# Rebuilding the last mixer tile and the router of a mixture-of-experts block, with unread matmuls between the router's steps

## The chip, the cores and the metric

The kernel runs on one core of a Trainium2 chip. The metric is the device time of one execution in microseconds, lower being better. Engines are named as in the profile: PE (TensorE matmuls), PEld (its weight loads), DVE (VectorE), ACT (ScalarE), POOL (GpSimd), SP (SyncE, which here only issues transfers).

## The reference, cut to what matters

One layer of an encoder, on x of 1024 tokens by 1024 channels, all in fp32. The part around the change:

```python
mix_out = jnp.einsum('bsd,de->bse', z, w_o[l])
x = x + gate_m[:, None, :] * mix_out
h2 = modulate(rms_norm(x, g_norm_moe[l]), shift_f, scale_f)      # h * (1 + scale) + shift
moe_out = expert_choice_moe(h2, w_router[l], ...)
x = x + gate_f[:, None, :] * moe_out
return rms_norm(x, g_final)

def expert_choice_moe(h, w_router, b_router, w_gate_e, w_up_e, w_down_e):
    probs = jax.nn.softmax(h @ w_router + b_router, axis=-1)     # 16 experts
    vals, idx = lax.top_k(jnp.swapaxes(probs, 1, 2), cap)        # each expert picks its 128 best tokens
    xe = h[idx]
    y = (jax.nn.silu(xe @ w_gate_e) * (xe @ w_up_e)) @ w_down_e  # 1024 -> 2048 -> 1024
    return scatter_add(y * vals)
```

No expert can start before every token's probability is known, since each picks its tokens from all 1024.

## The kernel before, in words

Every large product is done in three matmuls of fp32r operands: each operand is split into a rounded part (`hi`, a copy on ACT) and the rest (`lo`, a subtraction on DVE), and hi x hi, hi x lo, lo x hi are summed in PSUM (`split`, L92 and L93; `mm3`, `mm3x`).

The work around the change comes in this order.

**The mixer's last product** (`mix_out`): eight tiles of 128 tokens. A tile takes eight k steps of six matmuls of 512 columns (L105, L108, L111), both column halves in each step. Behind it the tile's x is added (L814), squared (L819), and stored; `rstd` goes over DVE and POOL (L656, L658); the row is scaled and modulated on DVE (L828, L830) and stored in `h2_d` by a POOL-issued transfer (L831). The router's work of a tile runs inside the next one, ahead of its k step 6: `turn` transposes x (L739) and splits it, `logits` multiplies with the router weights (L747, L749) and takes the softmax (L752 to L760), and `compare` ranks the tokens of experts 0 and 1 against all earlier ones (L859 to L878): comparisons on DVE, counted by small matmuls on PE (L862). For the last tile, 7, transposes and logits come after its own products.

**The router's end** (`run`): `compare` of tile 7 for expert 0, then `pick`: a one-hot table on DVE (L968), eight small matmuls (L975), the index (L981), and the gather of 128 rows of `h2_d` (L985) by an indirect POOL transfer. `turn` (the method) transposes the gathered rows (L1002) and splits them into `xh` and `xl`. The ranking of expert 1 and the search for the other 14 run as side work during expert 0.

**Sixteen experts** (`expert`): the weights come as units of 1 MB into a ring of raw buffers (`fetch`, L1018; 7 + 5 + 3 = 15 of them), and `unit` splits each in two halves of 1024 columns into `whi` and `wlo`, of which the pool `mwsp` has NWS = 3 each. The first three `wlo` are queued on DVE behind the index (L1037); all others go through `split`. An expert takes four column blocks: `up` twice (L1155 to L1157, gate and up), `put` (transposes of the product, L1077), `down` (L105 to L111). The next expert's gather is issued in the second block, its rows are turned between the two halves of the last `down`, and after that `ys` is scaled (L1126) and added into `x2_d` by an indirect transfer (L1127). After the last expert the rows are normalised (`final`).

The order on each engine isn't written out: the framework orders instructions by a simulated schedule with the traced order as priority, each engine then runs its queue in that order, and `issue_after(i)` queues what a block traces behind instruction i on i's engine. On the chip a waiting instruction holds up all behind it on its engine.

## Time and profile before

| | |
|---|---|
| median of 3 runs | 1964.37 us (1959.64 to 1964.53) |
| profiled execution | 1961.4 us, span 1959.6 us |
| PE busy | 1881.2 us (96%) |
| DVE busy | 1608.2 us (82%) |
| ACT busy | 1169.2 us (60%) |
| POOL busy | 141.7 us (7%) |
| mean granted clock of TensorE | 0.984 of full speed |
| HBM traffic | 549.03 MB, mean 280 GB/s |

Busy shares are of the span. The page's second part cuts the span into 40 slices of 49 us; PE shows 9 tenths in all but the first, the slice around 760 us, and the last. The mixer's product ends shortly before 754 us, the experts' products run from 783 to 1950 us. A busy PE isn't one at its peak, as matmuls are pipelined: distances from start to start tell more than durations.

### The profile page before, as it was taken

The numbers are of one execution on the slowest core, as the hardware profiler recorded it, in microseconds if no ns is written. First come the engines' busy times: TensorE is split into PE (matmuls) and PEld (weight loads), VectorE is DVE, ScalarE is ACT, GpSimd is POOL, SyncE is SP. The second block draws the span as 40 slices with busy tenths as digits, with TensorE's granted clock in tenths as the row PEclk, the third lists the DMA queues.
The fourth block names the chain that finished last, engine by engine and source line by source line (L and its number), as shares of the span: only waits on it lengthen the run. The fifth ranks groups of instructions, "written<-read, shape, count | busy, mean of one in ns | idle before, by whom it ended". The sixth has DMA issues, their size and how long they took to land.

```text
span 1959.6 us, 24141 instructions
## 1 busy us (share of the span) xinstructions
PE 1881.2 (96%) x8677; PEld 1505.6 (77%) x8677; DVE 1608.2 (82%) x2083; ACT 1169.2 (60%) x1402; POOL 141.7 (7%) x127
## 2 busy tenths in 40 slices
PE   6999999999999996999999999999999999999985
PEld 5788888777788874777888888777777877777764
DVE  5976669676753777999999999899999899998985
ACT  5533233433411422777777777777777777777784
POOL 1000000000131111000000000000000000000011
PEclk9999999999999997999999999999999999999997
DMA  8322224464764945999999999999999999999981
GB/s 296 128 65 65 86 86 151 160 223 171 258 240 121 328 148 208 361 327 375 373 369 384 376 370 356 384 363 356 387 359 360 381 365 361 381 369 350 378 309 79
DMA packets 245261, 549.03 MB, mean 280 GB/s; under 512 B 12644, under 2 KB 51652, under 8 KB 245140
## 3 DMA queue, kind: packets, MB, share of 16 engines
q1 hardware_dynamic: 230160, 496.07, 70.0%
q0 software_dynamic: 14128, 51.18, 8.2%
q8 instruction: 68, 1.11, 0.2%
q14 instruction: 53, 0.43, 0.1%
q10 hardware_dynamic: 852, 0.24, 0.1%
HBM read 507.61 MB, written 39.86 MB: 279 GB/s over the span
## 4 chain that ended last, share of the span: by engine, by line
PE 79%; DVE 10%; issue 6%; ACT 2%; DMA 1%; POOL 1%; POOLq 0%; SPq 0%; ACTq 0%; DVEq 0%
PE pb L314 9%; PE u L1157 6%; PE pa L314 6%; DVE wlo L93 6%; PE pc L314 6%; PE u L1155 6%; PE u L1156 6%; PE a L1157 5%; PE a L1156 4%; PE a L1155 4%; PE y L105 4%; PE y L108 4%; PE y L111 4%; PE mm L111 3%; PE mm L105 3%
## 5 line engine op out<-in xcount | busy, mean ns | idle before, releaser
L93 DVE TENSOR_TENSOR wlo<-raw,whi 128x1024 fp32r<-128x1024 f32 x765 | 912.1, 1225 | 64.9 <-ACT whi L92 52.4
L92 ACT ACTIVATE whi<-raw 128x1024 fp32r<-128x1024 f32 x765 | 803.1, 1060 | 216.0 <-PE y L111 78.1
L1157 PE MATMUL a<-wlo,xh 128*128 128x512 f32 x512 | 208.5, 407 | 10.3 <-DVE wlo L93 9.5
L1155 PE MATMUL a<-whi,xh 128*128 128x512 f32 x512 | 204.4, 399 | 6.8 <-ACT whi L92 6.8
L1157 PE MATMUL u<-wlo,xh 128*128 128x512 f32 x512 | 204.7, 400 | 2.4 <-DVE wlo L93 1.8
L1155 PE MATMUL u<-whi,xh 128*128 128x512 f32 x512 | 204.3, 399 | 0.2 <-ACT whi L92 0.2
L1156 PE MATMUL a<-whi,xl 128*128 128x512 f32 x512 | 203.4, 397 | 0.2 <-DVE xl L93 0.2
L1156 PE MATMUL u<-whi,xl 128*128 128x512 f32 x512 | 202.7, 396 | 0.0
L108 PE MATMUL y<-wlo,hth 128*128 128x512 f32 x508 | 162.6, 401 | 2.6 <-DVE wlo L93 2.6
L105 PE MATMUL y<-whi,hth 128*128 128x512 f32 x508 | 160.8, 397 | 2.4 <-ACT whi L92 2.4
L111 PE MATMUL y<-whi,htl 128*128 128x512 f32 x508 | 158.6, 393 | 0.0
L1157 PEld LDWEIGHTS a<-wlo,xh 128*128 128x128 f32 x512 | 97.0, 190 | 44.5 <-DVE wlo L93 23.3
L92 ACT ACTIVATE wh<-s 128x512 fp32r<-128x512 f32 x80 | 50.3, 631 | 134.9 <-PE pc L314 73.4
L1157 PEld LDWEIGHTS u<-wlo,xh 128*128 128x128 f32 x512 | 96.7, 189 | 28.9 <-DVE wlo L93 6.1
L1155 PEld LDWEIGHTS a<-whi,xh 128*128 128x128 f32 x512 | 97.5, 190 | 27.1 <-ACT whi L92 7.2
L1156 PEld LDWEIGHTS a<-whi,xl 128*128 128x128 f32 x512 | 97.4, 190 | 23.4 <-DVE xl L93 0.7
L1156 PEld LDWEIGHTS u<-whi,xl 128*128 128x128 f32 x512 | 96.7, 189 | 21.9
L1155 PEld LDWEIGHTS u<-whi,xh 128*128 128x128 f32 x512 | 96.8, 189 | 21.0 <-ACT whi L92 0.6
L111 PEld LDWEIGHTS y<-whi,htl 128*128 128x128 f32 x508 | 95.8, 189 | 21.0
L105 PEld LDWEIGHTS y<-whi,hth 128*128 128x128 f32 x508 | 93.8, 189 | 22.0 <-ACT whi L92 2.9
L108 PEld LDWEIGHTS y<-wlo,hth 128*128 128x128 f32 x508 | 92.0, 189 | 22.0 <-DVE wlo L93 4.5
L92 ACT ACTIVATE wh<-ld 128x512 fp32r<-128x512 f32 x68 | 42.4, 629 | 88.1 <-issue 36.1
(523 smaller groups left out, 3157.2 us busy)
## 6 DMA issues: line engine op xcount, KB each, us to landing
raw<-in_w_gate_e_dram SPq DMA_DIRECT2D x128, 1024.0 KB, 8.4
raw<-in_w_up_e_dram SPq DMA_DIRECT2D x126, 1024.0 KB, 7.6
raw<-in_w_down_e_dram SPq DMA_DIRECT2D x126, 1024.0 KB, 8.2
ld<-in_w_ada_dram SPq DMA_DIRECT2D x48, 512.0 KB, 5.0
ld<-in_w_in_dram SPq DMA_DIRECT2D x44, 512.0 KB, 4.6
sg_d<-q POOLq DMA_DIRECT2D x8, 1024.0 KB, 5.0
ld<-sg_d SPq DMA_DIRECT2D x16, 512.0 KB, 4.3
x<-in_x_dram SPq DMA_DIRECT2D x8, 512.0 KB, 5.1
```

Of the source, the lines that this page charges most:

```text
L92: self.nc.scalar.activation(hi, src, AF.Copy)
L93: self.nc.vector.tensor_tensor(lo, src, hi, op=OP.subtract)
L105: nc.tensor.matmul(o, lhsT=lh, rhs=rh, start=first, stop=False)
L108: nc.tensor.matmul(o, lhsT=lh, rhs=rl, start=False, stop=False)
L111: nc.tensor.matmul(o, lhsT=ll, rhs=rh, start=False, stop=last)
L314: nc.tensor.matmul(o, lhsT=x[:, k, :], rhs=y[:, k, :], start=first and k == 0 and i == 0, stop=last and k == 3 and i == 2, skip_group_chec ...
L1155: nc.tensor.matmul(o, lhsT=lhs[0], rhs=rhs[0], start=first, stop=False)
L1156: nc.tensor.matmul(o, lhsT=lhs[1], rhs=rhs[0], start=False, stop=False)
L1157: nc.tensor.matmul(o, lhsT=lhs[0], rhs=rhs[1], start=False, stop=last)
```

## The change

- **The last mixer tile** goes by column halves: 24 matmuls for columns 0 to 511, then 24 for the others. Its first half of x is added, squared, transposed and multiplied with the router weights inside the second half.
- **Router work spread**: in the other tiles the work for the tile before stands at three places, `side(0)` (compare of the tile before that), `side(2)` (turn), `side(4)` (logits and softmax), instead of all ahead of step 6. The router weights are negated, so that softmax needs no subtraction ahead of Exp. `compare` takes both experts at once, copies its row on ACT, and stops at a `yield` between the comparisons and the counts.
- **Rows unmodulated**: `h2_d` gets x times rstd, one ACT instruction (`norm`); for tile 7 SP issues both stores, the rows first. Scale and shift are applied after the gather, in the method `turn`, where they are one value per partition: for the first expert on ACT and DVE side by side straight from PSUM, for the others by four ACT instructions a half into `xf`, a copy to `xh` and a subtraction to `xl`.
- **Buffers**: `mwsp` has NWB = 6 of `whi` and `wlo` each; the raw ring is 7 + 4 + 1 = 12. NWS stays 3 where it says which `wlo` are queued behind the index.
- **Later**: `ys` and its scatter are traced after the first unit pair of the next expert (`left`); the load of `g_final` after the last expert's first `up`.
- **Unread matmuls**: `warm` issues n matmuls of the identity with itself, fp32, 128 columns, whose result nobody reads, queued behind a named PE instruction: 2, 5 and 10 at the end of `mix_out`, 4 and 7 around the counts of tile 7, 18 after the index's matmuls.

```diff
-NRA, NRB, NRC, NWO = 7, 5, 3, 6
-NWS = 3
+NRA, NRB, NRC, NWO = 7, 4, 1, 6
+NWS, NWB = 3, 6
...
+    def warm(self, psum, n):
+
+        t = psum()
+        with self.tc.issue_after(self.pe):
+            for _ in range(n):
+                self.nc.tensor.matmul(t[:, 0:P], lhsT=self.ident, rhs=self.ident, start=True, stop=True)
...
+        def norm(x2, h2, ss, ts, eng):
+            nc.vector.tensor_tensor(ss[:, 0:1], ss[:, 0:1], ss[:, 1:2], op=OP.add)
+            rs = self.rstd(pool, ss[:, 0:1], "y")
+            nc.scalar.activation(h2, x2, AF.Copy, scale=rs)
+            eng.dma_start(out=self.h2_d[ts, :], in_=h2)
+            self.afterld = eng.dma_start(out=self.x2_d[ts, :], in_=x2).ins
+            return rs
...
+            for n in range(2):
+                cs = slice(512 * n, 512 * n + 512)
+                for k in range(KD):
+                    if n == 0 and k % 2 == 0:
+                        side(k // 2)
+                    if n == 1 and k == 0:
+                        side(4)
+                    if n == 1 and k == 3:
+                        xt = turned()
+                        turn(x2, xt, 0)
+                    if n == 1 and k == 5:
+                        cmp = self.compare(t - 1, range(NCMP), psum)
+                        next(cmp)
+                    if n == 1 and k == 7:
+                        pl = psum()
+                        logits(pl, xt, 0)
+                    self.mm3([ps[:, cs]], (zh[:, k, :], zl[:, k, :]), [(self.wo[0][:, k, cs], self.wo[1][:, k, cs])],
+                             first=(k == 0), last=(k == KD - 1))
+                add_x(x2, ps, n)
+                if n == 0:
+                    sumsq(x2, h2, ss, n)
...
+            next(cmp, None)
+            self.warm(spare, 2)
+            turn(x2, xt, 1)
+            self.warm(spare, 5)
+            sumsq(x2, h2, ss, 1)
+            rs = norm(x2, h2, ss, ts, nc.sync)
+            logits(pl, xt, 1)
+            self.warm(spare, 10)
+            softmax(t, rs, pl)
...
-            self.split(xh[:, 4 * hf:4 * hf + 4, :], xl[:, 4 * hf:4 * hf + 4, :], pt)
+            hs = slice(4 * hf, 4 * hf + 4)
+            f = pool.tile([P, 4, P], F32, name="xf")
+            for k in range(4):
+                a, b = (self.vc[:, j + 4 * hf + k:j + 4 * hf + k + 1] for j in (16, 0))
+                if first:
+                    nc.scalar.activation(xh[:, 4 * hf + k, :], pt[:, k, :], AF.Identity, scale=a, bias=b)
+                    nc.vector.tensor_scalar(f[:, k, :], pt[:, k, :], a, b, op0=OP.mult, op1=OP.add)
+                else:
+                    nc.scalar.activation(f[:, k, :], pt[:, k, :], AF.Identity, scale=a, bias=b)
+            if not first:
+                nc.scalar.activation(xh[:, hs, :], f, AF.Copy)
+            nc.vector.tensor_tensor(xl[:, hs, :], f, xh[:, hs, :], op=OP.subtract)
...
+                if self.left:
+                    self.left.pop()()
...
-        gwsp, self.wsp = pool("mwsp", "right", bufs=NWS)
+        gwsp, self.wsp = pool("mwsp", "right", bufs=NWB)
...
-        self.compare(p, psum, ST - 1, 0)
+        cmp = self.compare(ST - 1, (0,), psum)
+        next(cmp)
+        self.warm(lambda: self.pau.tile([P, 512], F32, name="a"), 4)
+        for _ in cmp:
+            pass
+        self.warm(lambda: self.pau.tile([P, 512], F32, name="a"), 7)
```

## Rows read from the trace of the kernel before

**Rows 1.** Windows, one late expert: us, engines' busy (instructions), PEclk, DMA share, GB/s.

```profile
1283.50:1354.80 71.30, 70.47 (x322) 56.24 (x321) 64.65 (x64) 55.08 (x59) 3.30 (x2) 1.00 1.03 374
```

**Rows 2.** Page, part 5: line, engine, shapes, count | busy us, mean ns | idle.

```profile
L93 DVE TENSOR_TENSOR wlo<-raw,whi 128x1024 fp32r<-128x1024 f32 x765 | 912.1, 1225 | 64.9 <-ACT whi L92 52.4
L92 ACT ACTIVATE whi<-raw 128x1024 fp32r<-128x1024 f32 x765 | 803.1, 1060 | 216.0 <-PE y L111 78.1
```

**Rows 3.** Timeline, PE: start, us, engine, line, operation [idle before <-releaser].

```profile
753.12 0.63 PE L111 MATMUL mm<-woh,zl 128*128 128x512 f32 x2
...
783.70 0.80 PE L1156 MATMUL a<-whi,xl 128*128 128x512 f32 x1 [0.17 <-DVE xl L93]
...
786.69 0.39 PE L1157 MATMUL a<-wlo,xh 128*128 128x512 f32 x1
```

**Rows 4.** Two-microsecond windows in the router, columns as in rows 1.

```profile
758.00:760.00 2.00, 0.00 (x0) 0.00 (x0) 2.00 (x4) 0.90 (x1) 0.00 (x0) 0.79 1.03 346
...
774.00:776.00 2.00, 0.00 (x0) 0.00 (x0) 2.00 (x3) 0.00 (x0) 0.41 (x1) 0.50 0.04 17
```

**Rows 5.** Timeline, tile 7's rstd and second half, POOL, ScalarE and VectorE.

```profile
757.16 0.55 POOL L658 TENSOR_TENSOR yrs<-yms,neghalf 128x1 f32<-128x1 f32 x1 [7.78 <-DVE yms L656]
757.36 0.60 ACT L92 ACTIVATE hth<-mm 128x512 fp32r<-128x512 f32 x1 [0.26 <-PE mm L739]
...
758.55 0.68 DVE L93 TENSOR_TENSOR htl<-mm,hth 128x512 fp32r<-128x512 f32 x1
```

**Rows 6.** Timeline, counts of tile 6 and probabilities of tile 7.

```profile
760.22 0.32 PE L862 MATMUL sm<-onesb,cmp 128*128 128x1 bf16 x6 [2.90 <-DVE cmp L859]
...
768.32 0.23 DVE L760 TENSOR_SCALAR prob<-lg,se 128x16 f32<-128x16 f32 x1
```

**Rows 7.** Timeline, index and gather of expert 0.

```profile
773.72 0.16 DVE L981 SCALAR_TENSOR_TENSOR idx<-r 128x1 int32<-128x1 f32 x1
...
775.59 1.60 POOL L985 DMA_INDIRECT xg<-h_d,idx  x1 [7.12 <-DVE res L892]
```

**Rows 8.** Chain that ended last, from 740 to 810: start, us, what.

```profile
767.90 6.65 DMA h_d<-h
...
775.59 4.95 DMA xg<-h_d,idx
```

**Rows 9.** Timeline, fp32 matmuls of 128 columns among others at full clock.

```profile
40.95 3.08 PE L142 MATMUL sm<-diag,x 128*128 128x128 f32 x24
```

**Rows 10.** Line 985, the gathers of all experts.

```profile
DMA to landing us min/median/max: 4.9/7.9/9.0
```

**Rows 11.** ScalarE by groups (columns as rows 2), 641 to 654.

```profile
L92 ACT ACTIVATE zh<-ya 128x128 fp32r<-128x128 f32 x2 | 0.5, 302 | 5.0 <-DVE ya L610 5.0
```

**Rows 12.** PE's waits, 600 to 760: us in total, times, longest.

```profile
PE mm L105 <- ACT zh L92: 1.1, 1, 1.1
```

**Rows 13.** Timeline, first unit of two experts, late and early pattern.

```profile
1356.84 0.39 PE L1155 MATMUL a<-whi,xh 128*128 128x512 f32 x1
1357.08 0.40 PE L1156 MATMUL a<-whi,xl 128*128 128x512 f32 x1
1358.13 0.50 PE L1157 MATMUL a<-wlo,xh 128*128 128x512 f32 x1 [0.66 <-DVE wlo L93]
...
1075.24 0.39 PE L1156 MATMUL a<-whi,xl 128*128 128x512 f32 x1
1075.81 0.50 PE L1157 MATMUL a<-wlo,xh 128*128 128x512 f32 x1 [0.18 <-DVE wlo L93]
```

**Rows 14.** Timeline, turn for the next expert, early (with its first matmul), late.

```profile
1068.58 1.04 PE L1002 MATMUL tp<-ident,xg 128*128 128x128 f32 x8
...
1072.22 0.40 PE L1155 MATMUL a<-whi,xh 128*128 128x512 f32 x1
...
1349.44 0.60 PE L1002 MATMUL tp<-ident,xg 128*128 128x128 f32 x4
```

**Rows 15.** Timeline, last expert.

```profile
1910.56 0.79 PE L1155 MATMUL a<-whi,xh 128*128 128x512 f32 x1 [6.76 <-ACT whi L92]
```

More of the change, by code (lines that the diff above doesn't have):

```diff
@@ new lines, in side @@
+        def side(n):
+            if prev is None:
+                return
+            t, x2, rs = prev
+            if n == 0 and t:
+                for _ in self.compare(t - 1, range(NCMP), psum):
+                    pass
+            if n == 2:
+                hold["xt"] = turned()
+                for hf in range(2):
+                    turn(x2, hold["xt"], hf)
+            if n == 4:
+                pl = psum()
+                for hf in range(2):
+                    logits(pl, hold["xt"], hf)
+                softmax(t, rs, pl)
@@ L801, in mix_out @@
             ps = self.psm.tile([P, D], F32, name="mm")
-            for k in range(KD):
-                if k == 6 and prev is not None:
-                    logits(t - 1, prev[1], *turn(prev[0]))
-                    for e in range(NCMP):
-                        self.compare(self.cmpp, lambda: self.pss.tile([P, 512], F32, name="sm"), t - 1, e)
-                self.mm3([ps[:, 0:512], ps[:, 512:1024]], (zh[:, k, :], zl[:, k, :]),
-                         [(self.wo[0][:, k, n:n + 512], self.wo[1][:, k, n:n + 512]) for n in (0, 512)],
-                         first=(k == 0), last=(k == KD - 1))
@@ L856, in compare @@
         pc = psum()
-        if t:
-            m = pool.tile([P, (ST - 1) * P], BF16, name="cmp", bufs=2)
-            nc.vector.tensor_scalar(m[:, 0:n], self.prow[:, e, 0:n], p, 0.0, op0=OP.is_ge, op1=OP.add,
-                                    accum_out=cnt[:, 0:1])
-            for i in range(t):
-                nc.tensor.matmul(pc[:, P + i:P + i + 1], lhsT=m[:, i * P:(i + 1) * P], rhs=self.onesb[:, 0:1],
-                                 start=True, stop=True)
-        nc.tensor.transpose(pc[:, 0:P], p.to_broadcast([P, P]), self.ident)
@@ L877, in compare @@
-        nc.vector.tensor_tensor(place[:, t:t + 1], place[:, t:t + 1], cnt[:, 1:2], op=OP.add)
-        last = nc.vector.tensor_tensor(place[:, t:t + 1], place[:, t:t + 1], cnt[:, 2:3], op=OP.add)
-        if t == ST - 1:
-            self.after = last.ins
-            nc.vector.tensor_copy(self.pos[:, :, e], place)
+        row = pc[:, 0:ne * P].rearrange("p (e s) -> p e s", e=ne)
+        num = pc[:, 256:256 + 8 * ne].rearrange("p (e t) -> p e t", e=ne)
+        p = [self.prob[:, t, e:e + 1] for e in es]
@@ new lines, in compare @@
+        for i in range(ne):
+            self.pe = nc.tensor.transpose(row[:, i, :], p[i].to_broadcast([P, P]), self.ident).ins
+        if not last:
+            nc.scalar.activation(self.prow[:, e0:e0 + ne, n:n + P], row, AF.Copy)
+        ms = []
+        for i, e in enumerate(es):
+            w = n if last else n + P
+            m = pool.tile([P, (ST - 1) * P], BF16, name="cmp", bufs=2)
+            nc.vector.tensor_scalar(m[:, 0:w], self.prow[:, e, 0:w], p[i], 0.0, op0=OP.is_ge, op1=OP.add,
+                                    accum_out=cnt[:, 0, i:i + 1])
+            ms.append(m)
@@ new lines, in compare @@
+        for i, e in enumerate(es):
+            own = pool.tile([P, P], BF16, name="own", bufs=2)
+            r = row[:, i, :] if last else self.prow[:, e, n:n + P]
+            nc.vector.scalar_tensor_tensor(own, in0=r, scalar=p[i], in1=self.upper, op0=OP.is_equal, op1=OP.mult,
+                                           accum_out=cnt[:, 1, i:i + 1])
+            if last:
+                own = pool.tile([P, P], BF16, name="own", bufs=2)
+                nc.vector.tensor_scalar(own, r, p[i], 0.0, op0=OP.is_ge, op1=OP.add, accum_out=cnt[:, 2, i:i + 1])
@@ new lines, in compare @@
+        yield
+        for i in range(ne):
+            for j in range(t):
+                self.pe = nc.tensor.matmul(num[:, i, j:j + 1], lhsT=ms[i][:, j * P:(j + 1) * P],
+                                           rhs=self.onesb[:, 0:1], start=True, stop=True).ins
+        if t:
+            nc.vector.tensor_tensor(place[:, :, 0:t], place[:, :, 0:t], num[:, :, 0:t], op=OP.subtract)
+        own = place[:, :, t]
+        if last:
+            nc.vector.tensor_tensor(cnt[:, 0, :], cnt[:, 0, :], cnt[:, 2, :], op=OP.add)
@@ L883, in weights3 @@
+        nc.vector.tensor_tensor(cnt[:, 0, :], cnt[:, 0, :], cnt[:, 1, :], op=OP.subtract)
+        self.after = nc.vector.tensor_tensor(own, own, cnt[:, 0, :], op=OP.add).ins
     def weights3(self, pool, e0, e1):
@@ L1326, in run @@
                 next(side)
-        picked = self.turn(mp, *picked)
+        picked = self.turn(mp, *picked, first=True)
+        self.left = []
         for e in range(NE):
```

204 lines of the change are left out of this document (100 added, 104 removed).

## The prediction

> **What bounds the kernel now.** I read the page's first two parts, then two-microsecond windows around their dip, then the timeline and the chain of waits there, last the expert stage by windows and timeline. TensorE is the bound nearly everywhere: its tenths stand at nine but for the dip around 760 and the last slices. In the expert stage (783 to 1950) a late expert takes 71.3 us, of which PE is busy 70.47 and VectorE 64.65 [rows 1]; nearly all of VectorE's and ScalarE's time goes to splitting weights, 1.225 and 1.060 us for each half unit [rows 2]. So PE sets the pace, with a few small stalls. The dip is the router: the last mixer matmuls start at 753.12 and end at 753.75 (call it T0); the first expert's second matmul, the first that needs `xl`, starts at 783.70, T0 + 29.95 [rows 3]. Between them runs one serial chain, with PE mostly waiting; the granted clock is 0.79 in 758 to 760 and 0.50 in 774 to 776 [rows 4]: TensorE sits at 1.2 instead of 2.4 GHz when the experts begin. From 783.70 to 786.69 [rows 3] it starts 7 matmuls, where 0.23 us apart (the distance at full clock in rows 13) would take 1.6: 1.4 us lost to the clock.
>
> **The chain before.** The last copy and subtraction of tile 7's transposed half end at 759.23, POOL's power for rstd beside them [rows 5]. Then PE waits 2.90 us for the comparisons of tile 6, whose counts stand ahead of tile 7's logits, and the probabilities end at 768.55, T0 + 14.8 [rows 6]. Ranking and picking end with the index at 773.88, T0 + 20.1; the gather starts only at 775.59 [rows 7], because the store of the modulated rows was issued at 767.90 and took 6.65 us; the gather itself took 4.95 [rows 8], with the DMA engines all but idle at its start (share 0.04) [rows 4].
>
> **The change, router part.** Times from T0', the new end of the last mixer matmul.
> T0' moves later: 4 transposes, 2 of compare, 8 logits matmuls of tile 7 and some 5 of tile 6 that trailed T0 now come before it: 19 instructions at no more than 0.128 us (an fp32 matmul instruction of 128 columns at full clock, 3.08 / 24 [rows 9]) are 2.4; most have fewer columns, so I take 2.1.
> Step 1: compare of tile 6 now stands in front of the add, and VectorE works in order. Its two long and two short comparisons end between 0.15 (the latency of the add's own matmul) and 0.85 after T0'; I take 0.85, as they are traced first. Add 0.68, as long as the subtraction of the same width [rows 5]: 1.55. Four transposes and their latency 0.6, copy 0.60, subtraction 0.68 [rows 5]: 3.5. Eight logits matmuls at most 1.0: 4.6.
> Step 2, beside it: Square and its sum 0.8 after the copy, two tiny steps, POOL 0.55 [rows 5]: rstd at 4.65. Softmax: three short VectorE steps of 0.23 at most [rows 6], then Exp behind the new scaling of the row (1024 columns, 1.06 [rows 2], traced ahead of it), two short steps: probabilities at 6.6, 8.2 earlier than before.
> Step 3: ranking and picking take 5.33 before (768.55 to 773.88) [rows 6, 7]; the small copy of places goes, unread matmuls add 0.3 (below), the order of the few adds changes: 5.0 to 5.3, index at 11.6 to 11.9.
> Step 4: six buffer pairs for split weights instead of three. Only the first three weight subtractions are held behind the index; the next three, 1.225 each [rows 2], may fall into gaps of this chain. Bounds 0 and 3.7; I take 1.3, since the gaps they fill are partly idle: 13.1.
> Step 5: the row store goes out at about 5.8, first on SP's queue, so the 1.7 us before the gather vanish. But x2's store, four weight units and gf follow on that queue: some 5.2 MB, 15 us at the 346 GB/s of such a prefetch [rows 4], still moving at 13. The gather took 4.95 alone; over all 16 it has 4.9/7.9/9.0 (min, median, max) [rows 10], the others beside weight traffic. I take 7.9: 21.0.
> The Trainium skill (DMA: Bandwidth & Descriptors, Queues, rings and completion order) says that each DMA engine goes round the queues that hold work, so POOL's queue gives the gather no priority; 7.9 against 4.95 agrees.
> Step 6: turn of the first expert: transposes 0.6, four 128-column activations of 0.302 [rows 11] with VectorE's twins beside them, subtraction 0.69: 2.6, so the second matmul is at T0' + 23.6.
> Unread matmuls: 46 calls of two instructions, as fp32 matmuls are here, 0.26 us a call [rows 9]: the batches of 2, 5, 10, 4, 7, 18 take 0.5, 1.3, 2.6, 1.0, 1.8, 4.6. Their covers are the waits above (about 1, 1.4, 2.0, 1.2, 1.8, 8): at full clock they cost 0.3. They keep PE busy to about T0' + 17; then 4 us stay empty, so I count the clock as half saved: 0.7 of 1.4.
> Sum: 29.95 - 23.6 - 2.1 + 0.7 = 5 us gained. Bounds: 10.5 (add at once, no fillers, gather 4.95, full clock) and about 0 (all fillers, gather 9.0, clock lost).
>
> **Mixer tiles 0 to 6.** Four VectorE instructions a tile and three broadcast loads go, one ScalarE scaling comes. PE is the bound there and waits for ScalarE 1.1 us once, for a split behind a load [rows 12]: between 0 and 1.1, I take 0.5 gained. The stores of x2 and rows now both wait for rstd in POOL's queue: nobody reads them before the gather.
>
> **Experts.** At a boundary PE waits for `wlo`: 1357.08 to 1358.13 is 1.05 where 0.23 is usual, so 0.82; in the early pattern 1075.24 to 1075.81, 0.34 [rows 13]. Read alike over the stage: five times 0.34, ten times about 0.8, twice 0.25 more in seven experts, 1.6 in expert 1: 14 us or somewhat more. The cause: three buffers, about 4 us of PE work, against xl, ys and h together on VectorE. Six double the lead, and ys moves behind the next expert's first unit; VectorE has the slack to build the lead (64.65 of 71.3 [rows 1]). So up to 14 gained.
> Against it: the turn. Before, two copies of 0.6 on ScalarE. Now per half four activations of 0.302 [rows 11], a copy of 0.6, and a single buffer `xf`, which the second half may write only after VectorE's subtraction of the first; behind that wait, on in-order ScalarE, stand weight splits, and behind them PE. In all 0.4 + 1.2 + 0.6 + (0 to 1.2 until VectorE is free) + 0.7 + 1.2 + 0.6 + 0.7 = 5.4 to 6.6 to the last `xl`. In the early pattern the transposes start at 1068.58 and the next expert at 1072.22 [rows 14]: the first half is needed after 3.9 (takes 2.9 to 4.1), the second after 6.7. With a split of 1.06 in between, a stall of 0 to 1.5. In the late pattern the first half's transposes start at 1349.44 [rows 14], 7.4 us before the seventh matmul of the next expert at 1356.84 [rows 13], so some 6 before its first: nearly nothing. I take 0.45 x 15 = 7 lost. Net 7 gained; bounds 14 gained and 8 lost.
> The Trainium skill (VectorE: DVE Perf Modes, section on the TRN2 errata) wants tiles of 512 elements or more, as each ScalarE or VectorE instruction pays a fixed cost; by its table four 128-column activations from PSUM would take 1.0 us (an estimate), 1.2 by the row. It speaks against this turn.
>
> **Tail.** PE stands 6.76 us for `whi` at 1910.56 [rows 15], ScalarE being busy with final norms. Three more half units ahead are worth up to 4.2 us of PE, but the ring shrinks from 15 to 12, so the x2 rows load later and the norms start later. Between 5 gained and 3 lost; 1.5 gained.
>
> **Sum.** 5 + 0.5 + 7 + 1.5 = 14 off the profiled execution's 1961.4: 1947.4. The median of the runs is 3.0 above that execution: 1950.
>
> **The rivals.**
> Everything fits (20%): the lead removes all stalls, the turn is hidden, gather and clock go well: 9 + 1 + 13 + 4 = 27: 1937. For it: VectorE's slack and the late pattern; against it: the prefetch beside the gather.
> The turn eats the lead (16%): the experts gain nothing, the rest 7: 1957, and 1961 if the router gives little. For it: 5.4 to 6.6 us of turn with 3.6 before the next expert.
> The unread matmuls become the chain (10%): if the clock falls all the same, a call takes twice 0.26, the batches of 5, 10, 4, 7 overrun their covers by about 1, 3, 1, 2 us, and the router gains nothing: 1955. This is also the case in which the addition doesn't do what it says. Against it: no gap ahead of the gather is as long as the 4 us after T0 that went before the 0.79 of [rows 4].
> Slower (9%): the stall at the boundary is 2.6 us instead of 0.45, as splits of 1.06 sit in ScalarE's queue between the halves and VectorE comes two subtractions late; 15 x 2.6 = 39 lost against 5 + 0.5 + 14 + 1.5 = 21 gained: 1982. From 1.4 a boundary nothing is gained, from 1.8 it is slower by over 0.3%. Against it: whatever ScalarE waits for, six pairs carry PE 8 us.
>
> **How the numbers follow.** Forecast 1950, 45%, own range 1943 to 1957. About 0.3%, 6 us, is what a measurement of this kernel can tell from no change, so faster is below 1958.5. The forecast, the first rival and about half of the second and third are there: 0.78; within 0.3%: 0.13; slower: 0.09. The range 1937 to 1963 leaves out the lower half of the first rival and the slow one, about 2 in 10.
>
> **What would show it.** Right: some 24 us from the last mixer matmul to the second expert matmul, a gather of over 7, PE's clock at 1.00 through most of the router, `wlo` waits of PE under 3 us in the expert stage, experts of about 70 us. Wrong: PE waiting for `xl` or `xh` at each boundary (the turn), VectorE doing `wlo` between Exp and index (fillers), chain steps standing behind unread matmuls, or experts still at 71.3 with the same stalls.

## The result, and the profile after

| | before | after |
|---|---|---|
| median, measured together | 1963.5 us | 1995.5 us (1993.0 to 1998.5) |
| ratio | 1 | 1.0167, 95% interval 1.0144 to 1.0191 |
| span of the profiled execution | 1959.6 us | 1991.2 us |
| PE busy | 1881.2 us | 1908.3 us |
| DVE busy | 1608.2 us | 1572.7 us |
| ACT busy | 1169.2 us | 1184.9 us |
| mean granted clock | 0.984 | 0.986 |

The kernel became slower by 1.7%, where 1950 us, 14 less than before, was forecast. The two profiles differ by 31.6 us. Cut at four events of PE, they differ here:

| stretch | before | after | difference | forecast |
|---|---|---|---|---|
| start to the first mixer matmul (code unchanged) | 639.8 | 641.6 | +1.8 | 0 |
| first to the end of the last mixer matmul | 113.9 | 122.8 | +8.8 | +1.6 |
| from there to expert 1's first matmul (router, expert 0) | 104.6 | 102.6 | -2.0 | -7.1 |
| experts 1 to 14 | 995.7 | 1017.7 | +22.0 | -7 |
| expert 15 and the end | 105.6 | 106.6 | +0.9 | -1.5 |

The first line is variation between executions: over all kernels of this study, which are alike up to there, the first mixer matmul starts between 639.1 and 646.2. So stages are compared below by distances inside a profile.

**The experts.** Windows of the changed kernel over one early expert (the third) and one late one (the ninth); the columns and the late expert of before are in [rows 1].

```profile
940.70:1012.20 71.50, 70.53 (x321) 56.52 (x321) 65.96 (x64) 57.89 (x67) 3.88 (x2) 1.00 1.04 381
1372.50:1445.80 73.30, 71.49 (x321) 56.10 (x320) 64.12 (x64) 54.27 (x67) 3.62 (x2) 1.00 0.99 358
```

Before, the same experts took 70.0 and 71.35 us. PE has no more work to do; it waits. In the early expert it waits for the turn, at the first two matmuls (timeline of PE):

```profile
1012.17 0.50 PE L1249 MATMUL a<-whi,xh 128*128 128x512 f32 x1 [0.35 <-ACT xh L1089]
1013.52 0.50 PE L1250 MATMUL a<-whi,xl 128*128 128x512 f32 x1 [0.61 <-DVE xl L1090]
```

In the late one it waits for `wlo`, not for the turn. The boundary after the ninth expert, timelines of ScalarE, VectorE and PE, in order of time:

```profile
1440.56 1.50 ACT L1087 ACTIVATE xf<-tp,vc 128x128 f32<-128x128 f32 x4 [2.15 <-PE tp L1078]
1441.94 1.06 ACT L92 ACTIVATE whi<-raw 128x1024 fp32r<-128x1024 f32 x1
1443.04 1.22 DVE L93 TENSOR_TENSOR wlo<-raw,whi 128x1024 fp32r<-128x1024 f32 x1 [2.46 <-ACT whi L92]
1444.32 0.72 PE L108 MATMUL y<-wlo,hth 128*128 128x512 f32 x2 [0.54 <-DVE wlo L93]
1449.89 0.50 PE L1251 MATMUL a<-wlo,xh 128*128 128x512 f32 x1 [1.04 <-DVE wlo L93]
```

ScalarE waits 2.15 us for the transposes, then does four activations of the turn, and only then the next weight copy. VectorE has waited 2.46 for that copy, and PE waits behind VectorE. Six pairs of buffers are there, but they are not filled: ScalarE's waits from 1300 to 1850 (us in total, times, longest) are all of one kind, a wait for a result that PE has yet to produce; none is for a buffer or for a load.

```profile
ACT hth L92 <- PE tp L1166: 68.9, 30, 4.5
ACT h L1191 <- PE a L1251: 59.2, 31, 3.0
ACT xf L1087 <- PE tp L1078: 14.9, 7, 2.1
```

The two groups of [rows 2] say the same: ScalarE's idle time before weight copies was 216.0 us and is now 77.0, most of it in both kernels until PE had read a buffer for the last time; VectorE's wait for the copies rose from 52.4 to 80.5.

```profile
L93 DVE TENSOR_TENSOR wlo<-raw,whi 128x1024 fp32r<-128x1024 f32 x765 | 904.0, 1223 | 84.6 <-ACT whi L92 80.5
L92 ACT ACTIVATE whi<-raw 128x1024 fp32r<-128x1024 f32 x765 | 769.1, 1059 | 77.0 <-PE y L111 28.9
```

**The mixer.** Tile 1 took 13.4 us before and takes 20.6 (last matmul to last matmul). Timelines of POOL, VectorE and PE:

```profile
652.05 0.57 POOL L611 DMA_DIRECT2D z_d<-ya  x1 [14.06 <-DVE ya L610]
659.61 0.18 DVE L782 COPY vc<-sm 128x24 f32<-128x24 f32 x1 [3.28 <-DMA z_d<-ya]
660.34 2.00 PE L793 MATMUL sm<-wsf,ones 128*128 128x16 f32 x16 [3.19 <-DVE wsf L786]
```

The copy into `vc` waits for a store of the stage before: `vc` moved to the pool that takes over the memory of `ya`, whose store lands 7.5 us after its issue. PE stands behind it in the middle of the tile, and its clock falls (0.83 from 660 to 670).

**The router.** The last mixer matmul ends at 764.41, T0'. Timelines, in order of time; [rows 3] and [rows 6 to 8] are their counterparts.

```profile
764.02 0.39 PE L111 MATMUL mm<-woh,zl 128*128 128x512 f32 x1
770.19 0.24 DVE L768 TENSOR_SCALAR prob<-lg,se 128x16 f32<-128x16 f32 x1
774.70 0.16 DVE L1057 SCALAR_TENSOR_TENSOR idx<-r 128x1 int32<-128x1 f32 x1
775.63 1.34 POOL L1061 DMA_INDIRECT xg<-h_d,idx  x1 [8.15 <-DVE v L962]
784.61 1.09 PE L1078 MATMUL tp<-ident,xg 128*128 128x128 f32 x4 [6.01 <-DMA xg<-h_d,idx]
791.99 0.80 PE L1250 MATMUL a<-whi,xl 128*128 128x512 f32 x1 [0.28 <-DVE xl L1090]
```

Probabilities at T0' + 6.0 and index at T0' + 10.4, both better than forecast; rows gathered at T0' + 20.2; but the matmul that needs `xl` is at T0' + 27.6. From the first transposes to it pass 7.4 us. Timelines of ScalarE and VectorE there:

```profile
785.73 0.46 ACT L1084 ACTIVATE xh<-tp,vc 128x128 fp32r<-128x128 f32 x1 [10.09 <-PE tp L1078]
786.22 0.41 DVE L1085 TENSOR_SCALAR xf<-tp,vc 128x128 f32<-128x128 f32 x1 [6.41 <-ACT xh L1084]
786.55 1.14 DVE L932 TENSOR_SCALAR_CACHE_REDUCE cmp<-prow,prob 128x896 bf16<-128x896 f32 x1
786.67 0.46 ACT L1084 ACTIVATE xh<-tp,vc 128x128 fp32r<-128x128 f32 x1 [0.48 <-DVE xf L1085]
788.18 1.21 DVE L93 TENSOR_TENSOR wlo<-raw,whi 128x1024 fp32r<-128x1024 f32 x1
```

The two engines go in turns on one transposed bank, each waiting for the other, and between its turns VectorE puts in a comparison and, ahead of the first `xl`, two weight subtractions of 1.21 us (at 788.18 and 789.63). The Trainium skill (PSUM — Partial Sum Buffer, Terms) says that two engines must not touch one bank at a time; the rows agree, as no two of the turn's steps here overlap. The clock, in windows of ten microseconds:

```profile
770.00:780.00 10.00, 8.42 (x84) 7.95 (x82) 9.13 (x24) 5.65 (x6) 2.91 (x3) 1.00 1.02 400
780.00:790.00 10.00, 3.64 (x18) 2.27 (x18) 3.76 (x9) 2.08 (x5) 0.00 (x0) 0.58 1.04 394
790.00:800.00 10.00, 8.49 (x34) 6.17 (x34) 8.71 (x25) 5.34 (x8) 0.00 (x0) 0.74 0.44 151
```

The unread matmuls hold it at 1.00 up to 780; PE then idles in the gather and the turn, and the experts begin at half speed, as in [rows 4].

### The profile page after: what moved, and what is told of

It is laid out like the page before. It is cut to its first block, busy times and chain, and to the rows that moved or that the text cites. A ratio compares the mean times of both kernels' runs of the same rounds, so it can differ in the third digit from the quotient of the medians.

```text
span 1991.2 us, 24122 instructions
## 1 busy us (share of the span) xinstructions
PE 1908.3 (96%) x8769; PEld 1515.8 (76%) x8769; DVE 1572.7 (79%) x1978; ACT 1184.9 (60%) x1543; POOL 145.1 (7%) x124
## 4 chain that ended last, share of the span: by engine, by line
PE 78%; DVE 8%; issue 6%; ACT 3%; DMA 3%; POOL 1%; ACTq 0%; POOLq 0%; DVEq 0%
PE pb L314 8%; PE u L1251 5%; PE pa L314 5%; PE pc L314 5%; PE u L1250 5%; PE u L1249 5%; PE y L108 5%; PE y L105 5%; PE y L111 5%; DVE wlo L93 5%; PE a L1251 4%; PE a L1250 4%; PE a L1249 4%; PE mm L105 3%; PE mm L108 3%
## 5 line engine op out<-in xcount | busy, mean ns | idle before, releaser
L93 DVE TENSOR_TENSOR wlo<-raw,whi 128x1024 fp32r<-128x1024 f32 x765 | 904.0, 1223 | 84.6 <-ACT whi L92 80.5
L92 ACT ACTIVATE whi<-raw 128x1024 fp32r<-128x1024 f32 x765 | 769.1, 1059 | 77.0 <-PE y L111 28.9
L1251 PE MATMUL a<-wlo,xh 128*128 128x512 f32 x512 | 209.1, 408 | 13.4 <-DVE wlo L93 11.7
```

Of the source, the lines that this page charges most:

```text
L92: self.nc.scalar.activation(hi, src, AF.Copy)
L93: self.nc.vector.tensor_tensor(lo, src, hi, op=OP.subtract)
L1251: nc.tensor.matmul(o, lhsT=lhs[0], rhs=rhs[1], start=False, stop=last)
```

## The experiments

Times are medians; each ratio is to the kernel before, run beside the experiment. T0' is the end of the last mixer matmul in each kernel. Code is cut to the lines that matter.

**1. `vc` among the constants.**

```diff
-        self.vc = pool.tile([P, 24], F32, name="vc")        # router_consts
+        self.vc = self.cpool.tile([P, 24], F32, name="vc")  # run, in the constants
```

> The changed kernel with one tile moved: `vc`, the shift and scale columns, lies in the pool of constants that lives through the whole kernel, instead of in the pool that takes over the merge stage's memory. Theory: the first mixer tiles end 10.7 us later than before the change, 7.7 of them in tile 1, because the copy into `vc` waits 3.3 us for the store of z from `ya`, whose memory it reuses, with the router-weight matmuls of PE behind it and the clock falling in that wait. Then tile 1 takes about 14 us like tile 0, and the whole gains between 3.3 (the wait alone) and 7.7: about 1989 us against 1995. Rival: the copy only shows a wait that a late load or transpose would impose anyway (the columns come from memory in the same moment): the wait moves to another releaser and the time stays within 2 us of 1995.

1990.5 us, ratio 1.0137 (1.0120 to 1.0154). The mixer takes 117.8 us instead of 122.8, tile 1 15.6 instead of 20.6. Timelines of VectorE and PE:

```profile
653.57 0.17 DVE L782 COPY vc<-sm 128x24 f32<-128x24 f32 x1
655.06 1.85 PE L793 MATMUL sm<-wsf,ones 128*128 128x16 f32 x16
```

No wait is left and no other took its place. Of the mixer's 8.8 us, 5.0 are this tile's memory.

**2. The old turn for experts 1 to 15;** their modulation is left out.

```diff
+            if not first:
+                self.split(xh[:, hs, :], xl[:, hs, :], pt)
+                continue
             f = pool.tile([P, 4, P], F32, name="xf")
```

> The changed kernel, but the turn of experts 1 to 15 is the old one: xh and xl straight from the transposes, two ScalarE copies and two VectorE subtractions per expert, no modulation (the rows of experts 1 to 15 stay unmodulated, so this part of the computation is left out). Expert 0 keeps its modulated turn. Theory: the turn's eight 128-column activations and its two extra copies stand in ScalarE's in-order queue among the weight copies, and the six buffers don't help in the late experts because the order on ScalarE holds no more weight copies ahead of each PE-bound step than before. Then late experts fall from 73.3 to about 71.4 and early ones from 71.5 to about 70.0, some 10 x 1.9 + 4 x 1.5 = 25 us: about 1970. Rival: the 12-deep ring or the moved scaling of ys sets the 73.3; then late experts stay above 72.5 and the time above 1983.

1975.0 us, ratio 1.0054 (1.0036 to 1.0072). Windows over an early and a late expert:

```profile
1017.40:1087.40 70.00, 70.00 (x322) 56.65 (x321) 65.86 (x65) 55.49 (x58) 3.88 (x2) 1.00 1.03 379
1371.40:1442.80 71.40, 70.84 (x322) 56.28 (x321) 64.16 (x64) 51.57 (x59) 3.63 (x2) 1.00 1.01 366
```

As the theory had it, the turn costs 1.5 us in an early expert and 1.9 in a late one. In all it is 20.5 us where 25 was expected; 2.2 of the difference are in expert 1, with a wait of 1.5 us for the one-hot table of the next pick. And without the turn six pairs, with `ys` moved, give a late expert nothing: 71.4, against 71.35 with the three pairs of before.

**3. The buffers of before.**

```diff
-NRA, NRB, NRC, NWO = 7, 4, 1, 6
-NWS, NWB = 3, 6
+NRA, NRB, NRC, NWO = 7, 5, 3, 6
+NWS, NWB = 3, 3
```

> The changed kernel with the buffers of before: three pairs of split weights and a ring of 15 raw units (7, 5, 3) instead of six and 12. Theory: six pairs give nothing in the late experts, and what decides when the late order begins is the stock of raw units: in this kernel's instruction order it begins at expert 8 instead of 5. Late experts stay at 73.3, early ones (2 to 7) lie at 71.5 to 72.0, so three experts gain 1.5 to 1.8 each and the rest may lose 0.5 in the early ones: 1988 to 1995. Rival: the six buffers carry part of the turn's stall after all; then late experts rise above 74.5 and the time above 2003.

2004.8 us, ratio 1.0217 (1.0193 to 1.0241): above the theory's range. The time is the rival's, but late experts don't rise, as the rival had it. Windows, early and late expert:

```profile
1019.60:1092.40 72.80, 70.97 (x321) 56.40 (x321) 66.11 (x64) 57.75 (x67) 3.88 (x2) 1.00 1.01 362
1529.70:1602.90 73.20, 71.40 (x322) 56.09 (x321) 64.57 (x64) 57.65 (x67) 3.62 (x2) 1.00 0.99 360
```

Late experts are the same with three pairs or six, as the theory said. Early ones lose 1.3 each and expert 1 takes 78.8 instead of 73.7, where 0.5 at most was allowed for: there six pairs do carry part of the turn. The late pattern begins at expert 9 instead of 6 (by the turn; the expectation counted from the first step that changes), which gives back 0.4 to 0.7 in three experts only.

**4. No unread matmuls.** `warm` returns at once.

> The changed kernel without any of the 46 unread matmuls. Theory: they stand in waits of the chain and cost it about 0.3 us; without them the granted clock falls between the chain's steps and PE's own steps there (transposes, logits, counts, picking) take up to twice as long, some 1 to 2 us, while the clock at the start of expert 0 stays as low as it is with them, since the gather and the turn leave PE idle for 10 us in either case: 1995 to 1998, the end of the index 0.5 to 2 us later after the last mixer matmul than the 10.4 with them. Rival: the unread matmuls stand in front of chain steps and hold them up: then the index comes 1 us or more earlier and the time falls by as much.

1993.3 us, ratio 1.0153 (1.0131 to 1.0175), within the interval of the changed kernel. The index is at T0' + 10.5, expert 1 begins at T0' + 102.7, where the changed kernel has 10.4 and 102.6. Two windows:

```profile
770.00:780.00 10.00, 1.15 (x16) 0.81 (x16) 8.94 (x23) 6.01 (x8) 2.91 (x3) 0.50 1.01 391
780.00:790.00 10.00, 3.36 (x18) 2.55 (x18) 4.87 (x12) 1.76 (x5) 0.00 (x0) 0.50 1.03 393
```

The time is below the theory's 1995 to 1998; nor does the index come earlier, which the rival wanted. The clock is at 0.50 in 770 to 780, where it was 1.00 with them. So they did what they were put in for, and in this kernel it is worth nothing that can be measured: the index comes at the same time, and by the time the experts begin the clock is as low in both. Experiment 12 shows another case.

**5. Weight splits forced ahead.** Each half is traced four halves before its use, and the steps that wait for PE are queued behind it (in short form):

```diff
+            while len(self.ready) <= AHEAD: next(self.halves, None)    # split a further half
+            with self.behind(0), self.behind(1):    # ScalarE, VectorE: after the last split
                 nc.scalar.activation(h, pa, AF.Silu)
                 nc.vector.tensor_tensor(h, pu, h, op=OP.mult)
```

and likewise around `put`'s split and the turn.

> The changed kernel with the weight splits forced ahead: each half unit's `whi` and `wlo` is traced four halves before its use, and on ScalarE and VectorE the steps that wait for PE (h, hth and htl, the turn) are queued behind the split of the fourth half ahead. Buffers, ring and turn as they are. Theory: in the late experts the instruction order on ScalarE holds the same few weight copies ahead of each PE-bound step as before the change, so six pairs are not filled; with four forced ahead the late waits for `wlo` (1.2 and 0.8 per expert) go, and late experts fall from 73.3 to the 71.5 of the early ones, where only the waits for xl and xh are left: about 17 us, 1978. Rival: ScalarE and VectorE can't get ahead in the late experts because of the turn's own work or because the loads arrive just in time; then late experts stay above 72.7 and the time above 1989.

2003.6 us, ratio 1.0220 (1.0185 to 1.0255): a miss. PE's waits for `wlo` in late experts are gone, all of them, but late experts take 74.8 us. PE's timeline at a boundary, and two windows from there on:

```profile
1451.07 0.50 PE L1270 MATMUL a<-whi,xh 128*128 128x512 f32 x1 [0.39 <-ACT xh L1091]
1453.79 0.50 PE L1271 MATMUL a<-whi,xl 128*128 128x512 f32 x1 [2.23 <-DVE xl L1092]
```

```profile
1451.10:1455.10 4.00, 1.77 (x7) 1.24 (x8) 4.00 (x5) 3.13 (x6) 2.32 (x1) 1.00 0.96 360
1455.10:1459.10 4.00, 4.00 (x12) 3.14 (x11) 3.75 (x4) 3.54 (x5) 0.00 (x0) 0.57 1.04 205
```

The turn now stands behind the splits, and its `xl` is 2.2 us late. That stall is followed by a granted clock of 0.57, which costs some 1.6 us more: one expert, number 10 counted from 0, had the same stall with the clock at 1.00 throughout and took 73.2. Expert 1 also takes 79.0 instead of 73.7, with a wait of 3.3 for `wlo`. So order cures the one wait, and the ten steps of this turn make the other.

**6. Modulation by GpSimd.** With `vc` among the constants and the old turn; some tiles share memory to make room:

```diff
+        if e:    # behind the gather
+            nc.gpsimd.tensor_tensor(xg, xg, self.a2, op=OP.mult)
+            nc.gpsimd.tensor_tensor(xg, xg, self.sf, op=OP.add)
```

> The changed kernel with `vc` in the pool of constants and the modulation of experts 1 to 15 done by GpSimd on the gathered rows (a product with and a sum of two broadcast rows, 1024 columns each, behind the gather), so that the turn is the old one: two ScalarE copies and two VectorE subtractions. Expert 0 keeps its modulated turn. The sum of two measured effects: 1995.5 - 5.0 (vc) - 20.5 (turn) = 1970, if GpSimd's two passes, some 2.4 to 2.7 us each by the same operation elsewhere in the trace, lie in its idle time between gather and turn; late experts 71.4, early ones 70.0. Rival: the passes slow VectorE's subtractions beside them or make the rows late for the turn: late experts above 72, the time above 1977.

2005.5 us, ratio 1.0219 (1.0186 to 1.0251): the rival. Timelines of POOL and VectorE in a late expert:

```profile
1408.40 2.72 POOL L1063 TENSOR_TENSOR xg<-xg,a 128x1024 f32<-128x1024 f32 x1 [7.74 <-DMA xg<-h_d,idx]
1411.20 3.29 POOL L1064 TENSOR_TENSOR xg<-xg,sf 128x1024 f32<-128x1024 f32 x1
...
1408.77 3.44 DVE L93 TENSOR_TENSOR wlo<-raw,whi 128x1024 fp32r<-128x1024 f32 x1
1412.13 0.68 DVE L93 TENSOR_TENSOR htl<-tp,hth 128x512 fp32r<-128x512 f32 x1
1412.73 2.84 DVE L93 TENSOR_TENSOR wlo<-raw,whi 128x1024 fp32r<-128x1024 f32 x1
```

The two weight subtractions beside GpSimd's passes take 3.44 and 2.84 us; the four before them and the three behind take 1.21 to 1.22. Each of the two ends 1.1 us after the pass beside it, as if it had stood until the pass was over. The subtraction between them, which reads one operand from PSUM (`tp`), takes its usual 0.68. The Trainium skill (GPSIMD Engine Reference, Specifications) says that GpSimd contends with VectorE instructions that have two SBUF inputs; the two slow ones have, and the rows agree. Late experts take 74.0 to 74.6; the early ones, which have a lead, stay at 70.0 to 70.5. Expert 1 also begins 5.9 us later after T0' than in the changed kernel, with PE waiting 3.8 in all for a mask of the token search.

**7. Expert 0's turn in wide steps.**

```diff
+                nc.vector.tensor_tensor(f, pt, a, op=OP.mult)    # 512 columns, a and b broadcast
+                nc.vector.tensor_tensor(f, f, b, op=OP.add)
+            nc.scalar.activation(xh[:, hs, :], f, AF.Copy)
```

> The changed kernel with expert 0's turn in wide steps: per half, VectorE multiplies and adds in two steps of 512 columns, ScalarE copies xh from that, VectorE subtracts; no two engines read the same transposed bank in turn. Theory: the 7.4 us from the first transposes of the gathered rows to the first matmul that needs xl come from ScalarE's and VectorE's eight 128-column steps each, which alternate on one PSUM bank; then it falls to about 4.5, the first such matmul from 27.6 to about 24.7 us after the last mixer matmul, and the whole by 3: 1992. Rival: what fills the 7.4 us is the other work in VectorE's queue (the comparison of expert 1 and two weight subtractions) and PE at half clock; then it stays above 6.5 and the time at 1995.

1992.8 us, ratio 1.0157 (1.0123 to 1.0191). Transposes to `xl`, timelines of PE and VectorE:

```profile
785.50 1.08 PE L1078 MATMUL tp<-ident,xg 128*128 128x128 f32 x4 [6.34 <-DMA xg<-h_d,idx]
790.10 0.80 PE L1250 MATMUL a<-whi,xl 128*128 128x512 f32 x1
790.84 1.21 DVE L93 TENSOR_TENSOR wlo<-raw,whi 128x1024 fp32r<-128x1024 f32 x1
```

4.6 us instead of 7.4, and expert 1 begins at T0' + 99.4 instead of 102.6. Then expert 1 takes 76.3 instead of 73.7, with a 1.5 us wait for the one-hot table of the next pick and new waits for `wlo`: most of the gain is given back, and the whole can't be told from the changed kernel. What the 2.8 us were isn't told apart here. The comparison still stands between the steps, but the two weight subtractions of 1.21, which stood there in the changed kernel, now come behind `xl` (the first at 790.84). Together they are 2.4, so the run doesn't show how much the narrow steps took and how much the work between them.

**8. Five weight units behind the gather.** The `issue_after(self.afterld)` loop goes; the loop behind the gather fetches `NRB + NRC`.

> The changed kernel with four weight units that were loaded from the end of the mixer on issued behind the gather instead, with the fifth, on GpSimd's queue. Theory: the gather takes 9.0 us because it shares the DMA engines with that prefetch (4.95 before the change, with idle engines); now the first transposes of the gathered rows come about 3.5 us earlier, 16.7 instead of 20.2 us after the last mixer matmul, and as seven units are in the ring, expert 0 doesn't wait for loads: 1992. Rival: the gather is late for its own reasons (the store of the rows that it reads, issued 6.9 us before it) or expert 0 then waits for its units: the transposes stay at 19 us or later, or the time doesn't fall.

1991.4 us, ratio 1.0145 (1.0114 to 1.0176). The window ahead of the gather, and PE's timeline where the rows arrive:

```profile
776.00:778.00 2.00, 2.00 (x25) 1.89 (x24) 1.48 (x5) 2.00 (x4) 0.00 (x0) 1.00 0.07 27
```

```profile
783.73 0.63 PE L1078 MATMUL tp<-ident,xg 128*128 128x128 f32 x4 [1.93 <-DMA xg<-h_d,idx]
```

With a DMA share of 0.07 before it the gather lands after 4.8 us; with 1.02, in the changed kernel, after 8.8. The transposes are at T0' + 16.1 instead of 20.2, expert 1 at 98.6 instead of 102.6. The late pattern begins one expert earlier, which gives back 1.6; the whole gain is at the edge of what is measured.

**9. Rows modulated at the store, as before,** all turns old, `vc` among the constants.

```diff
-            nc.scalar.activation(h2, x2, AF.Copy, scale=rs)
+            for i in range(2):
+                cs = slice(512 * i, 512 * i + 512)
+                nc.vector.scalar_tensor_tensor(h2[:, cs], in0=x2[:, cs], scalar=rs, in1=a2[:, cs],
+                                               op0=OP.mult, op1=OP.mult)
+                nc.vector.tensor_tensor(h2[:, cs], h2[:, cs], sf[:, cs], op=OP.add)
```

> The changed kernel with `vc` in the pool of constants and the rows modulated where the kernel before does it, on VectorE ahead of their store, so that every turn, expert 0's too, is the old one of two copies and two subtractions. Theory: the turn's 20.5 us and vc's 5.0 add up; expert 0's turn falls from 7.4 to about 3.3; against this stand 2 to 3 us for four VectorE steps of 512 columns in the last tile's chain and 0.5 in the other tiles: about 1969, late experts 71.4. That is still above the kernel before, because the late experts gain nothing from six pairs and the ring of 12 begins the late order one expert earlier. Rival: the 20.5 us were gained by leaving the modulation out, and come back wherever it is done: above 1980.

1964.6 us, ratio 1.0014 (1.0001 to 1.0026): better than expected by 4, and not the rival. Expert 0's turn takes 3.9, expert 1 begins at T0' + 100.1, late experts take 71.4. The steps ahead of the store cost less than the 2 to 3 allowed: the transposes of the gathered rows are at T0' + 21.4 against 20.2.

**10. The same with the splits forced ahead.**

> The same with the weight splits forced four halves ahead. With the order forced and the modulated turn in place the waits for `wlo` had gone in the late experts, but one of 2.2 us for xl took their place at each boundary. Theory: with the old turn nothing takes their place, and late experts fall from 71.4 to the 70.0 to 70.4 that PE needs: ten experts by 1.2, some 12 us, so about 1957, below the kernel before. Rival: any turn that is queued behind four forced splits is late at the boundary: then PE waits for xh or xl there by 1 us or more, and late experts stay at 71.2 or more, the time at 1968 or above.

1951.0 us, ratio 0.9944 (0.9925 to 0.9963), below the expected 1957. PE waits for nothing in experts 2 to 14. A late expert, and PE's timeline in expert 1:

```profile
1363.20:1433.20 70.00, 70.00 (x321) 56.54 (x321) 63.67 (x64) 53.73 (x59) 11.25 (x2) 1.00 1.03 375
```

```profile
911.22 0.37 PE L1062 MATMUL tp<-v,oh 128*128 128x5 bf16 x8 [5.39 <-DVE oh L1055]
```

13.6 us less than kernel 9, by order alone: experts 2 to 14 gain 12.5, expert 1 loses 4.0, and expert 15 with the end gains 5.0. In expert 1 PE waits 5.4 us, instead of 1.5, for the one-hot table of the next pick; VectorE is busy all that time (5.50 of 5.50 us), with weight subtractions between the steps of the token search that the table needs, and the clock then falls to 0.50.

**11. Kernel 10 with three pairs, two halves ahead, ring of 15.**

> The last kernel (rows modulated at the store, old turn, `vc` in the constants, splits forced ahead) with the buffers of before: three pairs and a ring of 15, so the splits can be forced only two halves ahead. It tells the order apart from the buffers. If the order alone decides, late experts stay at 70.0 and the time near 1951. If the six pairs are what the order needs, PE waits for `wlo` again after ys, xl and the steps of h, about as in the kernel before (0.3 to 0.8 us at a time, 1.3 per expert): late experts at 70.8 to 71.4, the time at 1960 to 1965. I expect the latter: three half units are about 4 us of PE, and VectorE has ys (1.3), xl (2 x 0.7) and a split of 1.2 in one run at the boundary.

1964.7 us, ratio 1.0009 (0.9997 to 1.0021). The time is as expected, half of the loss against kernel 10 from another place: late experts take 70.75, not 70.8 to 71.4, which with the early ones (70.4) is 7.7 us over experts 1 to 14; the other 7.0 are in the tail, where PE waits 6.7 for `whi` instead of 1.9. So both count: order takes late experts from 71.4 to 70.75, and six pairs with four halves ahead from there to 70.0. The number of pairs, the halves ahead and the ring change together here, so their shares aren't told apart.

**12. Kernel 10 with the five units behind the gather.**

> The last kernel, six pairs and four halves ahead, with the five weight units that follow the first seven issued behind the gather. In the changed kernel this brought the gathered rows about 4 us earlier, and 2 of them were lost again because the late order began one expert earlier. With the order forced nothing of that kind is left to lose: 3 to 4 us gained, 1947 to 1948. Rival: expert 0 or 1 waits for the loads that now start some 8 us later: 1951 or above.

1945.7 us, ratio 0.9906 (0.9889 to 0.9924), the best here. PE's timeline where the rows arrive, and a window there:

```profile
776.30 0.63 PE L1091 MATMUL tp<-ident,xg 128*128 128x128 f32 x4 [2.22 <-DMA xg<-h_d,idx]
```

```profile
776.00:778.00 2.00, 1.01 (x7) 0.65 (x7) 0.40 (x1) 0.60 (x1) 0.94 (x2) 1.00 1.02 399
```

The gather takes 5.0, expert 1 begins at T0' + 93.4 (99.5 in kernel 10), and experts 1 to 14 lose only 0.9 of that. The 6.0 us are more than the 3 to 4 expected. The transposes come 3.0 earlier, and the rest goes with the clock: the last unread matmuls end at 774.08, only 2.2 us before the transposes, and the granted clock stays at 1.00 through all of expert 0, where in kernel 10 it is 0.50 from 784 to 792. Here the unread matmuls may well pay; no kernel without them was run in this form.

## Why the prediction was wrong

**Experts: "Six double the lead ... so up to 14 gained".** This step failed, and its 14 us with it: without the turn (experiment 2) experts 1 to 14 take 998.9 us, 3.2 more than before. Weight copies are issued ahead of need only if they stand ahead in ScalarE's queue, and that order is fixed when the program is built. An expert uses 48 half units, and PE has consumed 46 of them when the turn for the next expert begins. The table gives the copies beyond these 46 that stand ahead of the turn's first step on ScalarE, counted in the order of its instructions in the traces:

```
turn for expert          1  2  3  4  5  6  7  8  9 10 .. 15
before                   3  3  3  3  3  3  0  0  0  0 ..  0
after                    6  6  6  6  6  0  0  0  0  0 ..  0
experiment 3 (3 pairs)   3  3  3  3  3  3  3  3  0  0 ..  0
experiment 10            6  6  6  6  6  4  4  4  4  4 ..  4
```

The two patterns that the prediction saw in the trace are these two orders. In the late one nothing stands ahead, whatever the number of buffers, so ten of the fifteen boundaries could gain nothing. The early ones, where six do stand ahead, had almost nothing to gain: they took 70.0 us before and take 70.0 with six pairs and the old turn, so the 0.34 read there was hardly lost time. Experiment 2 (late 71.4 with six pairs and the old turn), 5 (order forced: no wait for `wlo` in late experts) and 10 (70.0) show it. The stalls themselves were there: against the kernel before, experiment 10 takes 11.8 us out of experts 2 to 14, of which expert 1 gives back 5.8.

Had the prediction asked what bounds ScalarE's lead, [rows 2] would have misled it, since there most of the wait before weight copies is for buffers. The late stage by itself would have shown more. ScalarE's waits in the kernel before, 1300 to 1850:

```profile
ACT h L1102 <- PE a L1157: 17.5, 31, 0.6
ACT xh L92 <- PE tp L1002: 11.2, 15, 1.2
```

From 930 to 1210, in early experts, there is no such wait; all are for buffers.

Why the late order begins where it does stays open. It begins at the turn for expert 6 with 12 units and six pairs, and at 5 where loads start later (experiment 8); but with 15 units and three pairs it is 7 before the change and 9 in experiment 3, so the ring alone doesn't set it. That the loads run dry in the schedule from which the order is taken is argued only; on the chip, in the changed kernel, copies wait for a load eleven times, at most 0.65 us and all before 1120, when the order is still the early one.

**Experts: the turn, 0.45 each.** Mis-sized by nearly three times: 1.3 us of waits early, 1.3 more than before late, 20.5 in all by experiment 2 against 7. Four activations take 1.50 us, where four times 0.302 was summed. The working bounded the stall at 1.5 for the early pattern and took the late one as nearly free, because its transposes come 6 us ahead. But there the turn's steps delay the weight copies behind them on ScalarE, and with no lead in the order each delay reaches PE as a wait for `wlo`. As a sign of failure the prediction named PE waiting for `xl` or `xh` at each boundary; that is so in early experts alone. As a sign of being right it named waits for `wlo` under 3 us; over experts 2 to 14 they are 14.6, against 7.1 before. The slow rival named the place and part of the mechanism, the turn's steps and the splits in one queue with VectorE late, and gave 1982; what PE waits for in late experts is `wlo`, though. The objection to it, "six pairs carry PE 8 us", is the failed step above. Experiment 5 comes near that rival: 2.2 us for `xl` at each late boundary.

**Mixer: +1.6 against +8.8.** The last tile cost 2.2 more, where 2.1 was forecast. Not seen was the wait of `vc` on a store, 5.0 us (experiment 1): moving a tile to another pool was read as no change. Without it tiles 0 to 6 lose 1.6, where 0.5 gained was forecast. Tile 1 loses 2.2 of work that was moved there: it now holds 42 small matmuls of PE for the router, 21 before, and tile 2 holds 26 instead of 41 and is 1.3 shorter. The rest, 0.1 to 0.3 us a tile in tiles 3 to 6, wasn't traced.

**Router.** Steps 1 to 4 did better than forecast: logits ended at T0' + 4.3 (4.6), probabilities came at 6.0 (6.6), the index at 10.4 (13.1); the further weight subtractions, which step 4 counted at 1.3, fell behind the index, not before it. Step 5: the gather took 8.8 (7.9), and that it pays for the prefetch is shown by experiments 8 and 12 (4.8 and 5.0 with quiet engines). The rule of the Trainium skill cited in the prediction (DMA: Bandwidth & Descriptors, Queues, rings and completion order), that a DMA engine goes round the queues that hold work, agrees. Step 6 failed: 7.4 us for 2.6. It was summed as if ScalarE and VectorE worked side by side; they share a bank and alternate, and other work gets between. How much of the 7.4 is either isn't told apart (experiment 7). The old turn takes 3.9 there (experiment 9).

**The unread matmuls: 0.3 lost, 0.7 gained.** Right in size, both near nothing (experiment 4), but not for the reason given. The clock was not half saved but wholly lost: the stretch without PE work lasted from 778.6 to 784.6, and the turn's waits followed. In experiment 12, where that stretch is 2.2 us, the clock held.

**Tail: +0.9 against -1.5.** PE waits 5.83 for `whi` instead of 6.76 [rows 15], and the rest of the tail loses 1.9. The 4.2 that three more halves were worth came out only with the order forced: in experiment 10 that wait is 1.9, and expert 15 with the end takes 97.9 us instead of 105.6.

## What to carry to other kernels

In this kernel more buffers let an engine run ahead only where its queue already had the work ahead: before crediting buffers, count what stands in front of each step that waits for the consumer, at every place where the pattern changes. A step that is cheap beside slack is dear inside an in-order queue whose lead is nought, so put added steps where lead exists, or force the order first; here the order was worth 13.6 us, and the added turn cost 20.5. A forced order also pushes other work back: look at what the forced steps now stand in front of, as in expert 1 of experiment 10. When a tile changes its pool, look at what its new memory waits for.

## What was not expected of the hardware

- A stall of PE of 2.5 us at a boundary was followed by a fall of the granted clock, to a mean of 0.57 over four microseconds, in most late experts of experiment 5, so it cost 1.6 us beyond itself; in one expert the same stall left the clock at 1.00, as stalls of 0.5 to 1.2 us did in the changed kernel.
- GpSimd's elementwise passes over 1024 columns (2.72 and 3.29 us) held up the one VectorE subtraction of two SBUF inputs beside each: 3.44 and 2.84 us instead of 1.22. A subtraction with one input from PSUM kept its 0.68.
- The gather of 128 rows for expert 0 took 4.8 to 5.0 us with the DMA engines all but idle ahead of it (the kernel before, experiments 8 and 12), and 8.8 beside weight loads at a share of 1.02 (the changed kernel).
